# Attention of a two-layer hybrid block: program order on TensorE, maxima steps behind each head's scores, value products in groups of up to four key blocks

## Chip, cores, metric

One core of one Trainium2 chip runs the whole program in one launch. The metric is the time on the device in microseconds (us), the median of the runs shown. A run also has a profile: one execution taken by the hardware profiler, with the start and the duration of every instruction.

The engines are TensorE (PE in the rows; PEld is its weight load), VectorE (DVE), ScalarE (ACT), GpSimd (POOL) and SyncE (SP, which issues the DMAs here). Each works through its own queue in order; semaphores join them.

## What is computed

Two layers over 1024 latent tokens and 256 context tokens, model width 1024, fp32 inputs. Each layer normalizes and modulates its tokens, projects them, runs four head groups side by side (A: latent attention, B: global attention, C: windowed attention with a sink, D: a state-space scan), projects the result back and adds it. The change touches the three attention groups alone. For a block of queries they compute

```python
def one_block(q_blk):
    s = jnp.einsum('bqhgd,bkhd->bhgqk', q_blk, k).astype(jnp.float32) * scale
    p = jax.nn.softmax(s, axis=-1).astype(v.dtype)
    return jnp.einsum('bhgqk,bkhd->bqhgd', p, v)
```

followed by a gate. Context queries read context keys only; latent queries read both (group C reads the context and three neighbouring blocks of 128 keys, with a mask). In the second layer no output is wanted for the context tokens.

## The kernel before, in words

**Pairs and units.** `attention` goes through six pairs of heads in the order B, B, A, A, C, C (`pairs`; `br` is 1, 0 or 2). Each pair is worked in units of query tokens, `GROUPS`: unit 1 (256 to 767), unit 2 (768 to 1279) and, in the first layer only, unit 0 (the 256 context tokens). One call of `main` is one unit.

**A unit.** The keys come in blocks of 128: ten blocks for units 1 and 2 of A and B, seven for those of C, two for unit 0. For each block, `scores` makes the transposed scores of both heads (lines 1215 to 1223: three matmuls per head in A, two in B, three with the mask in C), each in a PSUM tile `ps_st` (tag S2, three buffers), and ScalarE turns each into probabilities `P` (line 1224; the two heads share one tile of the ring `bg`, six buffers, which other work uses too). `add` sums the probabilities over the blocks on GpSimd and VectorE (lines 1240 and 1246). `values` multiplies values by probabilities into `ps_acc` (line 1231): fp32, 64 columns of the array per head, head 0 in columns 0 to 63 and head 1 in columns 64 to 127.

**Order of the value products.** Blocks are gathered in batches of `BATCH` = 2. When a batch is full, the values of the batch *before* it are emitted (`flush_values`), so they lag by one batch; the last batch is emitted by `output` in the next unit.

**Maxima.** The exponential needs each query's largest score, which is computed ahead, by steps that `maxima` returns: `ctx_part` and `lat_part` (`scored`, lines 1143 to 1147: a matmul into `ps_s`, tag MX, three buffers, and a maximum on VectorE into `mp`), and at the end of a query group the step `end`: a reduction into `mt` on VectorE, a transposition `ps_m` on TensorE (line 1171), a copy `ng` on ScalarE and two small DMAs that put the negated maxima as a row into the query tile that line 1217 or 1223 reads. The maxima of units 2 and 0 are made during unit 1; those of the next pair's unit 1, with the loads of that pair (`prep`), during unit 2. These steps are the `pieces` of `main`. They are emitted after each block, evenly, and are to be finished `LEAD` = 2 blocks before the unit's last. In the last pair there are steps `late` besides, which load and split the output weights (`wo`) through the ring `bg`.

**Tail.** After its blocks a unit returns three steps for the next unit to run: `output` (the last values, copy of `ps_acc`, gate), the token sums (eight transpositions `ps_sum`, sixteen instructions on ScalarE, a reciprocal) and `finish` (a transposition `ps_rt`, a DMA out, two back, the product `y`). One is emitted with each batch.

**What sets the order.** The program text is not the order on the engines: a scheduler (the tile framework's) places the instructions of all five engines by its own estimates, as their inputs and buffers come free, and TensorE's queue is a result of that.

Of the kernel before, what the change touches and what calls it, by code (L numbers as in the profile page):

```python
# [24 lines left out]
LEAD = 2  # L25
RD = 2
RD2 = 0
BATCH = 2
N_LATE = 3
AFTER = 3  # L30
X_AT = 0
# [26 lines left out]
def hybrid_block(ctx, tc, x, ctxt, c_t, w_fm, w_tm, w_mod, b_gate, p_col, p_row, w_qu, w_kvu, w_out,  # L58
# [65 lines left out]
    def ps(tag, name=None):  # L124
        return pp.tile([P, 512], F32, tag=tag, bufs=PS_BUFS[tag], name=name or f"ps_{tag}")
# [910 lines left out]
    def attention(L, res, need_ctx, y, late):  # L1036
# [160 lines left out]
        def main(op, gi, pieces, tail):  # L1197
            lo, n = GROUPS[gi]
            nt = n // P
            br, kd = op["br"], op["kd"]  # L1200
            acc = ps("ACC", name="ps_acc")
            sums = [None]
            blocks = key_blocks(br, gi)

            def scores(bi):
                kb, c0, w, mo = blocks[bi]
                k = lambda tok, rows: tok.tile(kb, 0, rows)
                pts = bg((P, 2, 512), name="P")
                for h in range(2):
                    st = ps("S2", name="ps_st")[:, :w]  # L1210
                    q0, q1 = op["q"][h]
                    q = lambda tok, rows: tok(lo + c0, w, 0, rows)
                    if br == 0:
                        k0, k1 = op["k"][h]
                        mm(st, lhsT=k(k0, 96), rhs=q(q0, 96), start=True, stop=False)  # L1215
                        mm(st, lhsT=k(k1, 96), rhs=q(q0, 96), start=False, stop=False)
                        mm(st, lhsT=k(k0, 97), rhs=q(q1, 97), start=False, stop=True)  # L1217
                    else:
                        k0, k1 = op["k"][0]
                        mm(st, lhsT=k(k0, 128), rhs=q(q0, 128), start=True, stop=False)  # L1220
                        if mo is not None:
                            mm(st, lhsT=ident_r, rhs=mask_r[:, mo:mo + w], start=False, stop=False)
                        mm(st, lhsT=k(k1, 65), rhs=q(q1, 65), start=False, stop=True)  # L1223
                    nc.scalar.activation(out=pts[:, h, :w], in_=st, func=AF.Exp, scale=op["scale"])  # L1224
                return pts

            def values(bi, pts):
                kb, c0, w, mo = blocks[bi]
                for h in range(2):
                    v0 = h * 64 if br == 0 else op["pair"] * 64  # L1230
                    mm(acc[h * 64:h * 64 + 64, c0:c0 + w], lhsT=op["v"].tile(kb)[:, v0:v0 + 64], rhs=pts[:, h, :w],  # L1231
                       start=(bi == 0), stop=(bi == len(blocks) - 1))

            def add(bi, pts):
                kb, c0, w, mo = blocks[bi]
                if bi == 0:
                    sums[0] = pts
                elif bi == 1:
                    s = ac((P, 2, 512), name="ac")
                    nc.gpsimd.tensor_tensor(out=s[:, :, :n], in0=sums[0][:, :, :n], in1=pts[:, :, :n], op=ALU.add)  # L1240
                    sums[0] = s
                else:
                    s = sums[0]
                    for h in range(2):
                        eng = nc.vector if h == 0 and bi % 2 == 0 else nc.gpsimd
                        eng.tensor_tensor(out=s[:, h, c0:c0 + w], in0=s[:, h, c0:c0 + w], in1=pts[:, h, :w], op=ALU.add)  # L1246

            todo = []

            def flush_values():  # L1250
                for bi, pts in todo:
                    values(bi, pts)
                todo.clear()

            total, done = len(pieces), 0
            batch = []
            for bi in range(len(blocks)):
                pts = scores(bi)
                batch.append((bi, pts))
                add(bi, pts)  # L1260
                if len(batch) == BATCH or bi == len(blocks) - 1:
                    for _ in range(2 if len(tail) > 3 else 1):
                        if tail:
                            tail.pop(0)()
                    flush_values()
                    todo.extend(batch)
                    batch = []
                want = min(total, -(-total * (bi + 1) // max(1, len(blocks) - LEAD)))
                while done < want:
                    pieces[done]()  # L1270
                    done += 1
            if br == 2:
                for h in range(2):
                    hd = op["pair"] * 2 + h
                    es = tm(name="es")
                    nc.scalar.activation(out=es[64:65, :n], in_=f32(op["q"][h][1](lo, n, 64, 65)), func=AF.Exp,
                                         scale=HEAD_SCALE, bias=pr[64:65, PR_SINK + hd:PR_SINK + hd + 1])
                    nc.vector.tensor_tensor(out=sums[0][64:65, h, :n], in0=sums[0][64:65, h, :n], in1=es[64:65, :n], op=ALU.add)
            o = tm(name="o")
            last_unit = gi == gorder[-1]  # L1280

            def output():
                flush_values()
                nc.scalar.copy(o[:, :n], acc[:, :n])
                nc.gpsimd.tensor_tensor(out=o[:, :n], in0=o[:, :n], in1=op["gate"](lo, n), op=ALU.mult)
                if last_unit:
                    free_all(op["free"])


            ss = small([P, 8], "asum", "asum", 2)  # L1290

            def token_sums(h):
                pss = ps("TR", name="ps_sum")
                for t in range(nt):
                    nc.tensor.transpose(pss[:, t * P:(t + 1) * P], sums[0][:, h, t * P:(t + 1) * P], ident)
                for t in range(nt):
                    junk = tm((P, P), name="junk")
                    nc.scalar.activation(out=junk, in_=pss[:, t * P:(t + 1) * P], func=AF.Copy, scale=2.0,
                                         accum_out=ss[:, h * nt + t:h * nt + t + 1])
                if h == 1:  # L1300
                    nc.vector.reciprocal(out=ss[:, :2 * nt], in_=ss[:, :2 * nt])

            def finish():
                pr_ = ps("TR", name="ps_rt")
                nc.tensor.transpose(pr_[0:2 * nt, 0:P], ss[:, :2 * nt], ident)
                row = tm((8, P), name="rrow")
                nc.scalar.copy(row[0:2 * nt, :], pr_[0:2 * nt, 0:P])
                dr = d_rs[n_unit[0] % 4]
                n_unit[0] += 1
                nc.sync.dma_start(out=dr[0:2 * nt, :], in_=row[0:2 * nt, :])  # L1310
                rb = tm(name="rb")
                for h in range(2):
                    nc.sync.dma_start(out=rb[h * 64:h * 64 + 64, :n],
                                      in_=dr[h * nt:(h + 1) * nt, :].rearrange("t q -> (t q)").unsqueeze(0).to_broadcast([64, n]))
                nc.vector.tensor_tensor(out=y[br * 2 + op["pair"]](lo, n), in0=rb[:, :n], in1=o[:, :n], op=ALU.mult)
            return tail + [output, lambda: [token_sums(h) for h in range(2)], finish]

        sink8 = const([P, 4])
        nc.vector.tensor_scalar(out=sink8, in0=pr[:, PR_SINK:PR_SINK + 4], scalar1=8.0, scalar2=None, op0=ALU.mult)
# [10 lines left out]
        y_slots, tail = [], []  # L1330
        for i, (br, pair) in enumerate(pairs):
            op = ops[br, pair]
            if need_ctx and i == 0:
                pk = Slot([P, 4, NCTX], F32, "y_cx")
                y_slots.append(pk)
            if need_ctx and br == 2:
                pk = res["ssd"].y_slots[0]
            s = Slot([P, NLAT], F32, f"y{br}{pair}")
            y_slots.append(s)
            y[br * 2 + pair] = Tok(pk.t[:, br * 2 + pair - (2 if br == 2 else 0), :] if need_ctx else None, s.t)  # L1340
            for gi in gorder:
                pieces = []
                if gi == 1:
                    for g in gorder[1:]:
                        pieces += maxima(op, g)
                elif gi == 2 and i + 1 < len(pairs):
                    pieces = prep(*pairs[i + 1])
                if i + 1 == len(pairs):
                    pieces = pieces + sum((late() for _ in range(N_LATE)), [])
                tail = main(op, gi, pieces, tail)  # L1350
        while len(tail) > 2:
            tail.pop(0)()
        yield y_slots, tail

# [128 lines left out]
    for L in range(DEPTH):  # L1483
# [48 lines left out]
        y_slots, tail = next(gen[0])  # L1532
# [86 lines left out]
```

## Time and profile before

| | us |
|---|---|
| median of 3 runs | 1849.13 |
| lowest, highest run | 1848.83, 1856.71 |
| profiled execution, its own time | 1844.81 |
| span of its instructions | 1843.0 |
| attention of the first layer in that span | about 545 to 856 |
| attention of the second layer | about 1440 to 1745 |

How to read it: busy time is the time in which an engine has an instruction in flight; a matmul's end is modelled, and matmuls overlap, so that the distance from one start to the next says more of TensorE than durations do. Where the timeline merges equal instructions, "x8" is their count and the duration is that of the whole stretch. In brackets stands the idle time before an instruction, and who ended it. The granted clock is a share of TensorE's 2.4 GHz.

### The profile page before, as it was taken

How to read it: one execution, taken by the hardware profiler on the slowest of the kernel's cores; microseconds unless marked ns; L12 is line 12 of the kernel's file. 1: busy time of each engine (PE TensorE's matmuls, PEld its weight loads, DVE VectorE, ACT ScalarE, POOL GpSimd, SP SyncE). 2: the span in 40 equal slices, each digit the busy share in tenths (PEclk: the TensorE clock that was granted, in tenths of full speed). 3: DMA queues.
4: the chain of work that ended last, by engine and by line, in shares of the span. 5: the costliest groups of instructions: out<-in, count | busy, mean ns of one | idle time of the engine just before them, and what ended most of it. 6: DMA issues, size and time to landing. Idle time of an engine off the chain costs nothing.

```text
span 1843.0 us, 27921 instructions
## 1 busy us (share of the span) xinstructions
PE 1752.4 (95%) x9658; PEld 1329.2 (72%) x9658; DVE 1131.8 (61%) x2290; ACT 744.3 (40%) x2060; POOL 783.3 (43%) x735
## 2 busy tenths in 40 slices
PE   6999999999999999998999989999999999999898
PEld 4667888889975556565787768888998555566576
DVE  6867864373466655447546777753744766645953
ACT  5332433332224545556323333343332445455631
POOL 2322552132327766656224134531332576665522
PEclk9999999999999999999999989999999999999999
DMA  9474323255684332224411524231668623220521
GB/s 312 148 229 134 122 100 119 86 189 178 192 221 117 84 105 74 59 62 128 151 58 40 164 90 148 87 120 70 215 195 249 163 75 88 56 65 12 179 85 58
DMA packets 130397, 231.54 MB, mean 126 GB/s; under 512 B 13784, under 2 KB 74560, under 8 KB 130256
## 3 DMA queue, kind: packets, MB, share of 16 engines
q1 hardware_dynamic: 130256, 229.75, 40.2%
q8 instruction: 77, 1.26, 0.3%
q14 instruction: 64, 0.52, 0.1%
HBM read 161.15 MB, written 68.44 MB: 125 GB/s over the span
## 4 chain that ended last, share of the span: by engine, by line
PE 75%; DVE 11%; DMA 4%; issue 3%; POOL 3%; ACT 2%; SPq 0%; POOLq 0%; DVEq 0%; ACTq 0%
PE ps_acc L1231 10%; PE ps_fm L128 7%; PE ps_fm L130 7%; PE ps_fm L129 7%; PE ps_s L1143 6%; PE ps_o L129 3%; PE ps_o L130 3%; PE ps_o L128 3%; PE ps_st L1220 3%; PE ps_st L1223 3%; PE ps_tm L128 2%; PE ps_tm L130 2%; PE ps_tm L129 2%; PE ps_st L1215 2%; PE ps_st L1217 2%
## 5 line engine op out<-in xcount | busy, mean ns | idle before, releaser
L1246 POOL TENSOR_TENSOR ac<-ac,P 128x512 f32<-128x512 f32 (+3 forms) x248 | 310.8, 1274 | 134.8 <-ACT P L1224 114.5
L1147 DVE TENSOR_REDUCE mp<-ps_s 128x1 f32<-128x512 f32 (+3 forms) x428 | 260.7, 658 | 167.7 <-PE ps_s L1143 154.5
L1224 ACT ACTIVATE P<-ps_st 128x512 f32<-128x512 f32 (+3 forms) x456 | 238.0, 555 | 263.5 <-PE ps_st L1223 102.9
L128 PE MATMUL ps_fm<-hh,wfm_hi 128*128 128x512 f32 x576 | 234.3, 407 | 3.2 <-DVE kb L658 1.9
L130 PE MATMUL ps_fm<-hl,wfm_hi 128*128 128x512 f32 x576 | 231.3, 402 | 1.5 <-POOL hl L403 0.7
L129 PE MATMUL ps_fm<-hh,wfm_lo 128*128 128x512 f32 x576 | 229.9, 399 | 0.0
L128 PE MATMUL ps_tm<-wtm_hi,hh 128*128 128x256 f32 x512 | 146.5, 286 | 0.8 <-ACT va L870 0.6
L129 PE MATMUL ps_tm<-wtm_hi,hl 128*128 128x256 f32 x512 | 145.5, 284 | 0.0
L130 PE MATMUL ps_tm<-wtm_lo,hh 128*128 128x256 f32 x512 | 145.3, 284 | 0.0
L130 PEld LDWEIGHTS ps_fm<-hl,wfm_hi 128*128 128x128 f32 x576 | 109.2, 190 | 27.2 <-POOL hl L403 3.3
L128 PEld LDWEIGHTS ps_fm<-hh,wfm_hi 128*128 128x128 f32 x576 | 109.5, 190 | 26.5 <-ACT hf L399 3.3
L129 PEld LDWEIGHTS ps_fm<-hh,wfm_lo 128*128 128x128 f32 x576 | 109.6, 190 | 19.4 <-issue 0.8
L1240 POOL TENSOR_TENSOR ac<-P 128x1024 f32<-128x1024 f32 (+1 forms) x30 | 65.4, 2180 | 136.7 <-ACT P L1224 133.9
L128 PE MATMUL ps_o<-wo_hi,yh 128*128 128x512 f32 x288 | 113.3, 395 | 2.7 <-ACT yh L1373 2.7
L129 PE MATMUL ps_o<-wo_hi,yl 128*128 128x512 f32 x288 | 113.4, 394 | 0.5 <-DVE yl L1374 0.4
L130 PE MATMUL ps_o<-wo_lo,yh 128*128 128x512 f32 x288 | 112.9, 392 | 0.0
L1231 PE MATMUL ps_acc<-P,vt 128*64 128x512 f32 (+3 forms) x416 | 104.3, 542 | 0.0
L128 PEld LDWEIGHTS ps_tm<-wtm_hi,hh 128*128 128x128 f32 x512 | 98.1, 192 | 3.1 <-issue 1.6
L130 PEld LDWEIGHTS ps_tm<-wtm_lo,hh 128*128 128x128 f32 x512 | 98.2, 192 | 0.7 <-issue 0.4
L129 PEld LDWEIGHTS ps_tm<-wtm_hi,hl 128*128 128x128 f32 x512 | 98.2, 192 | 0.5
L1400 POOL TENSOR_TENSOR xres<-xres,dl 128x512 f32<-128x512 f32 x32 | 41.3, 1290 | 105.5 <-DVE dl L1399 105.5
L1246 DVE TENSOR_TENSOR ac<-ac,P 128x512 f32<-128x512 f32 (+3 forms) x88 | 64.8, 736 | 29.1 <-ACT P L1224 17.6
(345 smaller groups left out, 4150.4 us busy)
## 6 DMA issues: line engine op xcount, KB each, us to landing
wfm_raw<-in_w_fm_dram SPq DMA_DIRECT2D x36, 512.0 KB
wm<-in_w_mod_dram SPq DMA_DIRECT2D x64, 256.0 KB
d_q<-qkhl SPq DMA_DIRECT2D x18, 512.0 KB
wm<-in_w_mod_dram SPq DMA_DIRECT2D x16, 512.0 KB
d_gate<-th SPq DMA_DIRECT2D x32, 256.0 KB
wtm_raw<-in_w_tm_dram SPq DMA_DIRECT2D x16, 512.0 KB
qq<-d_q SPq DMA_DIRECT2D x32, 256.0 KB
wo_raw<-in_w_out_dram SPq DMA_DIRECT2D x16, 512.0 KB
```

The lines of the kernel that those rows point to most:

```text
L128: mm(o, lhsT=lh, rhs=rh, start=first, stop=False)
L129: mm(o, lhsT=ll, rhs=rh, start=False, stop=False)
L130: return mm(o, lhsT=lh, rhs=rl, start=False, stop=last)
L1143: mm(o, lhsT=qh(lo + t * P, P, 0, km), rhs=kh(k0, w, 0, km), start=True, stop=mo is None)
L1147: nc.vector.tensor_reduce(out=dst, in_=p[:, :nu * w].rearrange("p (u k) -> p u k", u=nu), axis=AX.X, op=ALU.max)
L1220: mm(st, lhsT=k(k0, 128), rhs=q(q0, 128), start=True, stop=False)
L1223: mm(st, lhsT=k(k1, 65), rhs=q(q1, 65), start=False, stop=True)
L1224: nc.scalar.activation(out=pts[:, h, :w], in_=st, func=AF.Exp, scale=op["scale"])
L1231: mm(acc[h * 64:h * 64 + 64, c0:c0 + w], lhsT=op["v"].tile(kb)[:, v0:v0 + 64], rhs=pts[:, h, :w], start=(bi == 0), stop=(bi == len(blocks) ...
L1240: nc.gpsimd.tensor_tensor(out=s[:, :, :n], in0=sums[0][:, :, :n], in1=pts[:, :, :n], op=ALU.add)
L1246: eng.tensor_tensor(out=s[:, h, c0:c0 + w], in0=s[:, h, c0:c0 + w], in1=pts[:, h, :w], op=ALU.add)
L1400: (nc.vector if t == ts[-1] else nc.gpsimd).tensor_tensor(out=xt.t[:, js], in0=xt.t[:, js], in1=d, op=ALU.add)
```

## The change

With the change, TensorE executes the instructions of each `main` in the order of the program text (`manual_schedule` for that engine alone); the other four engines are placed by the scheduler as before. The text is rewritten: the maxima steps are emitted after each head's scores (twice per block) rather than after each block; values are no longer held back by a batch, they follow the scores of the last block of their group; groups are as even as they can be at up to four blocks (ten blocks: 4, 3, 3; seven: 4, 3; two: 2); the tail has five steps, two of them empty, of which one is emitted after each block, two if more than five are waiting.

```diff
-BATCH = 2
+BATCH = 4
@@ scores
-            def scores(bi):
+            def scores(bi, between):
                     nc.scalar.activation(out=pts[:, h, :w], in_=st, func=AF.Exp, scale=op["scale"])
+                    between(2 * bi + h + 1)
@@ main
-            todo = []
-
-            def flush_values():
-                for bi, pts in todo:
-                    values(bi, pts)
-                todo.clear()
-
             total, done = len(pieces), 0
-            batch = []
-            for bi in range(len(blocks)):
-                pts = scores(bi)
-                batch.append((bi, pts))
-                add(bi, pts)
-                if len(batch) == BATCH or bi == len(blocks) - 1:
-                    for _ in range(2 if len(tail) > 3 else 1):
-                        if tail:
-                            tail.pop(0)()
-                    flush_values()
-                    todo.extend(batch)
-                    batch = []
-                want = min(total, -(-total * (bi + 1) // max(1, len(blocks) - LEAD)))
+
+            def between(step):
+
+                nonlocal done
+                want = min(total, -(-total * step // (2 * max(1, len(blocks) - LEAD))))
                 while done < want:
                     pieces[done]()
                     done += 1
+
+            nb = -(-len(blocks) // BATCH)
+            ends = [-(-len(blocks) * (b + 1) // nb) - 1 for b in range(nb)]
+            batch = []
+            for bi in range(len(blocks)):
+                pts = scores(bi, between)
+                batch.append((bi, pts))
+                add(bi, pts)
+                for _ in range(2 if len(tail) > 5 else 1):
+                    if tail:
+                        tail.pop(0)()
+                if bi in ends:
+                    for b in batch:
+                        values(*b)
+                    batch = []
@@ output, return of main
-                flush_values()
-            return tail + [output, lambda: [token_sums(h) for h in range(2)], finish]
+            return tail + [output, lambda: None, lambda: [token_sums(h) for h in range(2)], lambda: None, finish]
@@ attention
-                tail = main(op, gi, pieces, tail)
-        while len(tail) > 2:
+                with tc.manual_schedule(engines={mybir.EngineType.PE}):
+                    tail = main(op, gi, pieces, tail)
+        while len(tail) > 4:
             tail.pop(0)()
```

## Rows read from the trace of the kernel before

**Rows 1.** The page, busy time of each engine (share of the span, instructions).
```profile
PE 1752.4 (95%) x9658; PEld 1329.2 (72%) x9658; DVE 1131.8 (61%) x2290; ACT 744.3 (40%) x2060; POOL 783.3 (43%) x735
```
**Rows 2.** Stages: stretch, length, busy of PE, PEld, DVE, ACT, POOL; granted clock, DMA.
```profile
600.00:660.00 60.00, 60.00 (x266) 33.47 (x263) 35.76 (x60) 31.75 (x95) 42.95 (x32) 1.00 0.36 98
1620.00:1680.00 60.00, 60.00 (x282) 36.57 (x279) 27.46 (x49) 30.57 (x90) 38.83 (x30) 1.00 0.09 24
```
**Rows 3.** PE's waits in both attention stretches, the longest of each: us, times, longest.
```profile
PE ps_sum L1295 <- DVE mp L1147: 1.8, 1, 1.8
PE ps_rt L1305 <- DVE asum L1301: 2.7, 2, 1.6
```
**Rows 4.** Timeline of PE: one unbroken group of values, two blocks (start, us, what).
```profile
615.07 1.94 PE L1231 MATMUL ps_acc<-P,vt 128*64 128x512 f32 x8
616.93 0.73 PE L1143 MATMUL ps_s<-kk,qq 128*128 128x512 f32 x2
```
**Rows 5.** Timeline of PE: a group of the same size, broken by two transpositions.
```profile
619.37 0.40 PE L1220 MATMUL ps_st<-qq,kk 128*128 128x512 f32 x1
619.60 0.39 PE L1223 MATMUL ps_st<-ql,k 65*128 65x512 f32 x1
619.92 1.93 PE L1231 MATMUL ps_acc<-P,vt 128*64 128x512 f32 x6
621.78 0.27 PE L1171 MATMUL ps_m<-con,mt 128*8 128x128 f32 x1
...
622.10 1.07 PE L1231 MATMUL ps_acc<-P,vt 128*64 128x512 f32 x2
```
**Rows 6.** Timeline of DVE: maxima, an addition, and the reduction of `end`.
```profile
560.00 1.89 DVE L1147 TENSOR_REDUCE mp<-ps_s 128x1 f32<-128x512 f32 x3 [1.48 <-PE ps_s L1143]
561.81 0.68 DVE L1246 TENSOR_TENSOR ac<-ac,P 128x512 f32<-128x512 f32 x1
562.41 0.68 DVE L1147 TENSOR_REDUCE mp<-ps_s 128x1 f32<-128x512 f32 x1
563.13 0.18 DVE L1166 TENSOR_REDUCE mt<-mp 128x8 f32<-128x24 f32 x1
```
**Rows 7.** Timelines of PE and DVE: from a last maxima matmul to its transposition.
```profile
1513.51 0.50 PE L1143 MATMUL ps_s<-kk,qq 128*128 128x512 f32 x1
...
1515.48 0.27 PE L1171 MATMUL ps_m<-con,mt 128*8 128x128 f32 x1
...
1514.65 0.68 DVE L1315 TENSOR_TENSOR y<-rb,o 128x512 f32<-128x512 f32 x1
```
**Rows 8.** Timeline of ACT: exponentials of both widths, first and last token sum.
```profile
598.30 1.21 ACT L1224 ACTIVATE P<-ps_st 128x256 f32<-128x256 f32 x4 [2.08 <-PE ps_st L1223]
...
1496.31 3.05 ACT L1224 ACTIVATE P<-ps_st 128x512 f32<-128x512 f32 x6 [0.30 <-PE ps_st L1223]
...
1500.56 0.28 ACT L1298 ACTIVATE junk<-ps_sum 128x128 f32<-128x128 f32 x1
...
1502.31 0.34 ACT L1298 ACTIVATE junk<-ps_sum 128x128 f32<-128x128 f32 x1
```
**Rows 9.** Timelines of SP and PE: last load of a pair, its first use.
```profile
616.85 0.57 SPq L1050 DMA_DIRECT2D kl<-d_kr  x1
...
632.65 0.74 PE L1143 MATMUL ps_s<-kh_cx,qh 96*128 96x256 f32 x4
```
**Rows 10.** Last pair: timeline of DVE, and PE's longest wait from 835 to 905.
```profile
858.37 2.87 DVE L1522 TENSOR_TENSOR wo_lo<-wo_raw,wo_hi 128x512 fp32r<-128x512 f32 x2
...
PE ps_sum L1295 <- DVE ac L1278: 5.6, 2, 4.5
```
**Rows 11.** Timeline of PE after a wait, and the stage (columns as in rows 2).
```profile
814.64 1.80 PE L1295 MATMUL ps_sum<-con,ac 128*128 128x128 f32 x8 [1.80 <-DVE mp L1147]
816.37 2.83 PE L1231 MATMUL ps_acc<-P,pk 128*64 128x512 f32 x8
...
816.00:820.00 4.00, 4.00 (x17) 1.62 (x16) 1.36 (x4) 1.92 (x15) 0.98 (x2) 0.72 0.00 0
```

## The prediction

> **What bounds the kernel now.** I read the page first: TensorE is busy 95% of the span, no other engine over 61% [rows 1]. Then the busy time by stages: in attention TensorE is busy in 60.00 of 60.00 us in either layer, at a granted clock of 1.00, that is 2.4 GHz, while VectorE has 27 to 36 us, ScalarE 31, GpSimd 39 to 43 [rows 2]. Then TensorE's waits: 7 rows with 4.3 us in the first layer's attention, 5 rows with 6.7 us in the second's, of each the longest stands in front [rows 3]. So the 616 us of attention last as long as TensorE's queue, and the change can give only what shortens that queue: fewer or cheaper instructions, or less time between them. It takes no matmul away. Last I read the timeline of TensorE start to start, since a full busy share hides how the time is used.
>
> There the queue is dense but not at its best. A score matmul of 512 columns starts 0.23 us after the one before (619.37 to 619.60), but 0.32 us pass ahead of a group of values (619.60 to 619.92) [rows 5]. A group of two blocks takes 1.86 us (615.07 to 616.93) [rows 4] and would be 4 x 0.43 = 1.72 at the spacing of its inner starts (the two heads start together, in four pairs 0.43 us apart, which this row merges into "x8"). So entering and leaving a group costs 0.09 + 0.14, some 0.24 us. And where the scheduler cut a group in two, head 1 of a block runs without head 0: 1.86 us, then two transpositions, then 1.07 us [rows 5], against 1.86 for the whole.
>
> **The change, part by part.** *Groups.* Counted along that timeline there are 69 groups now in the first layer and 70 in the second, 139, whole as in the one row and cut as in the other [rows 4, 5]. With 4, 3, 3 blocks (4, 3 in group C, 2 in unit 0) and nothing between, the first layer has 4 x (3+3+1) + 2 x (2+2+1) = 38, the second 4 x 6 + 2 x 4 = 32: 70. 69 fewer x 0.24 = 16.6 us. *Lone heads.* 27 times a piece with one head alone stands in the queue, 20 of them with 512 columns. Each costs 0.43 us twice, since both heads then go alone: 20 x 0.86 + 7 narrower ones at about half of that = 20 us. In program order nothing can come between the two heads, so all of it goes. *Waits of today*: 11 us, replaced by those below. Gain: 16.6 + 20 + 11 = 47.6 us.
>
> The Trainium skill, TensorEngine Tiling (Array Packing), Key Properties, says that a change of tiling mode drains TensorE; going from 128x128 to 128x64 and back is such a change, and the rows agree that it costs something [rows 4, 5]. It names no price, so the sum goes by the rows.
>
> *The step `end`.* This is the price. Now its transposition is put wherever the scheduler finds room; in program order it stands behind the last maxima matmul, and TensorE waits with everything behind it: scores, values, and so ScalarE's exponentials. From the last maxima matmul to the transposition 1.97 us passed (1513.51 to 1515.48), 0.60 of them because of a product `y` on VectorE in between [rows 7]; that leaves 1.37: matmul 0.4, maximum 0.68, reduction 0.18 and the ways between [rows 6]. Of that TensorE works off what stands between. In the six cases where `end` follows its last maxima matmul directly (unit 1 of the first layer's pairs in A and B, and twice in its last pair), only 0.23 us do. There VectorE is late too: a maximum or an addition takes it 0.61 us (three and one in 560.00 to 562.41) [rows 6], at 1.6 maxima and a quarter of an addition per head 1.1 us, while TensorE needs 0.84 in B (two score matmuls and 1.6 maxima at 0.23) and 1.07 in A. After five heads of a group VectorE is 1.3 us behind in B. So 1.4 (A) to 2.5 us (B), 2.0 on the mean: 12 us. In the other 22, one head's scores (0.47 in B, 0.70 in A) stand between, and mostly two maxima are queued: 1.37 + 0.61 - 0.23 - 0.5 to 0.7, some 1.0: 22 us. Bounds: 0.6 and 1.9 for each of the 28, 17 to 53 us.
>
> *Three buffers of maxima.* Within a group's scores TensorE can be three maxima, 1.8 us, ahead of VectorE [rows 6]. Eight heads in B are 8 x (1.1 - 0.84) = 2.1 us behind, less the token sums' transpositions that fall there. I take 2 us in all; bounds 0 and 22 (0.7 in each of 32 stretches of scores in A and B).
>
> *Unit 0, six times.* Its four exponentials take 1.21 us [rows 8], its scores at 256 columns about half of that, and no lag of a batch covers them now: 0.6 us each, 3.6; bounds 0 and 4.
>
> *Tail.* Token sums come after block 2, `finish` after block 4, with an empty step between: 16 instructions on ScalarE take 2.1 us (1500.56 to 1502.65) [rows 8], one block and a group of values of 2.7 us and more are longer: nothing. After unit 0 two steps are taken per block, and one block (1.6 us) stands between the sums and `ps_rt`: 0.7 us, five times, 3.5; bounds 0 and 8. `finish`'s three DMAs go to SP's queue a block earlier; what waits for them is a product on VectorE off the path.
>
> *Loads.* `prep` comes after the first head; its loads go by free slots, and one pair's last stands 15.8 us ahead of its first use [rows 9]. Nothing; half a unit (12 us) of lead would have to be lost before it costs. The DMAs of `ng` have two blocks and a group of values, over 4.5 us, ahead of their reader; nothing.
>
> *Last pair.* VectorE splits output weights there (2.87 us for two) and TensorE's sums wait for the sink's addition behind it, 4.5 us at the longest [rows 10]. In order that holds up scores too: 3 us more; bounds 0 and 8.
>
> *Clock.* At 814.64 TensorE had been idle for 1.80 us; the group behind took 2.76 us instead of 1.86 and the stretch 816 to 820 shows a granted clock of 0.72 [rows 11], so the lower level, 1.2 GHz, for part of it. One such fall more, 1.7 us; bounds 0 and 14 (eight waits near 2 us).
>
> Sum of costs: 34 + 2 + 3.6 + 3.5 + 3 + 1.7 = 47.8; gain 47.6; net +0.2 us. On the profiled execution's 1844.81 us, whose span of 1843.0 leaves 1.8 around it, that is 1845.0. The median of the runs lies 4.3 us above that execution: 1849.3, so **1849 us**: no change that can be told.
>
> **The rivals.** *A, faster: the waits are covered.* If VectorE meets the last maxima idle, a wait is 1.37 - 0.23 - 0.5 = 0.6 us: 28 x 0.6 + 7 for the rest = 24 us, net -24: 1825. For it: VectorE is busy 46 to 60% of the stage, and each group of values (2.7 or 3.6 us without a maximum) lets it catch up [rows 2, 4]. Against it: two maxima are mostly emitted in the step ahead of `end`.
>
> *B, slower: VectorE falls behind in each stretch of scores.* Now its maxima are fed between groups of two blocks; with four blocks in a row the three buffers fill and TensorE, in order, stands. It decides from the point where VectorE's lag passes 1.8 us: with an addition that waits for GpSimd, or a `y` of 0.6 us, in a stretch. Then 32 x 0.7 = 22 us come on top, less the 2 counted: 1849 + 20 = 1869. For it: 2.1 us of lag in eight heads of B; against it: A has none. The Trainium skill, TensorE: Matmul & The Clock Gate, Part 3, states that matmuls start and end strictly in the order of the program, so no later one can slip past a waiting one; the rows here show no exception. Its Part 1 states that an idle array falls back to 1.2 GHz; each such fall is 1.7 us [rows 11], which would push this case to the upper bound.
>
> *C: the order does not hold what it says*, groups are still cut by work from outside `main`. Then the waits are filled as now, and half of the groups' 16.6 and of the lone heads' 20 us is gained: 1849 - 18 = 1831.
>
> **How the numbers follow.** Forecast 0.37, A 0.28, B 0.30, C 0.05. About 0.5%, 9 us, is what a measurement of this kernel can tell from no change. A and C are faster by more, B slower by more: 0.33, 0.37, 0.30. Low end: gain 47.6 against 17 + 2 of costs, 1849 - 28 = 1821. High end: B with five more falls of the clock, 1869 + 5 x 1.7 = 1877. So 1821 to 1877; the forecast's own range is 1840 to 1858.
>
> **What would show it.** Groups "x12" to "x16" of values on TensorE, about 70, none with "x2"; idle time ahead of `ps_m` whose releaser is `mt`, 28 us or more in sum; idle time ahead of `ps_s` from `mp` (B) near 2 or 20 us; a granted clock under 1.00 within attention; scores of unit 0 followed by a gap. I am wrong if `ps_m` does not wait (A), or if TensorE's idle time in attention passes 60 us (B).

## The result, and the profile after

The changed kernel takes 1880.22 us (median of four runs, 1879.48 to 1882.64) against 1850.53 for the kernel before beside it: a ratio of 1.0161, 95% interval 1.0139 to 1.0182. It is slower by about 30 us. The prediction was 1849 with a range up to 1877; direction and size were both missed.

The page of the changed kernel, its span, the busy times, and the granted clock in 40 slices:

```profile
span 1880.7 us, 27918 instructions
PE 1742.3 (93%) x9658; PEld 1345.2 (72%) x9658; DVE 1138.1 (61%) x2290; ACT 749.1 (40%) x2060; POOL 776.2 (41%) x735
PEclk9999999999999999998999989999999999999899
```

Against [rows 1], TensorE is busy for 10 us less in a span that is 37.7 us longer, and the clock has two more slices under 9. (The two profiled executions lie further apart than the medians do, 37.7 us against 29.7: the one before is a quick one of its kernel, 1844.81 us, the one after is the slowest of its four.) The busy time by stages says where. First before, then after; each row is one layer's attention, from the last `ps_fm` matmul ahead of it to the first `ps_o`, and PEclk is the granted clock:

```profile
core 0: us, PE busy (x) PEld busy (x) DVE busy (x) ACT busy (x) POOL busy (x), PEclk, DMA share, GB/s
541.80:876.90 335.10, 322.38 (x1529) 195.04 (x1527) 204.60 (x350) 176.01 (x538) 213.08 (x159) 0.99 0.35 95
1435.70:1744.70 309.00, 300.73 (x1366) 176.72 (x1365) 202.07 (x316) 154.84 (x437) 197.74 (x148) 0.99 0.31 84
```

```profile
544.90:906.50 361.60, 319.63 (x1528) 200.09 (x1526) 212.27 (x349) 178.51 (x538) 205.67 (x159) 0.95 0.32 86
1469.10:1783.20 314.10, 287.50 (x1369) 182.02 (x1368) 202.35 (x319) 158.67 (x443) 197.48 (x148) 0.97 0.31 86
```

The first layer's attention is 26.5 us longer, the second's 5.1: 31.6 of the 37.7 us. (The other 6 lie outside attention and were not followed.) In these two stages TensorE's busy time falls by 16.0 us and its idle time rises from 21.0 to 68.6, by 47.6. So there is a gain in work, and a larger loss in waiting.

TensorE's waits in the same two stages of the changed kernel, first layer and then second (us in total, times, longest); they answer to [rows 3]:

```profile
PE ps_m L1171 <- DVE mt L1166: 16.2, 10, 3.1
PE ps_m L1171 <- DVE mt L1169: 10.9, 6, 2.5
PE ps_sum L1295 <- DVE ac L1279: 4.5, 2, 2.5
PE ps_st L1223 <- DMA ql<-ng: 2.1, 1, 2.1
...
PE ps_sum L1295 <- DVE ac L1279: 8.6, 3, 4.2
PE ps_m L1171 <- DVE mt L1166: 6.1, 8, 1.5
PE ps_m L1171 <- DVE mt L1169: 5.2, 4, 1.8
PE ps_st L1223 <- DMA ql<-ng: 2.2, 1, 2.2
```

The transposition of `end` (`ps_m`) waits 38.4 us in sum. Before, it waited 1.2 us in both stages, 0.5 in the first layer and 0.7 in the second, most of it here:

```profile
PE ps_m L1171 <- DVE mt L1169: 0.5, 1, 0.5
PE ps_m L1171 <- DVE mt L1166: 0.4, 1, 0.4
```

One of the longest waits after, in the timeline, VectorE first, then TensorE:

```profile
562.86 0.88 DVE L1247 TENSOR_TENSOR ac<-ac,P 128x512 f32<-128x512 f32 x1
563.66 2.47 DVE L1147 TENSOR_REDUCE mp<-ps_s 128x1 f32<-128x512 f32 x4
566.18 0.69 DVE L1247 TENSOR_TENSOR ac<-ac,P 128x512 f32<-128x512 f32 x1
566.79 0.17 DVE L1166 TENSOR_REDUCE mt<-mp 128x8 f32<-128x24 f32 x1
```

```profile
563.65 0.40 PE L1143 MATMUL ps_s<-kk,qq 128*128 128x512 f32 x1
567.11 0.37 PE L1171 MATMUL ps_m<-con,mt 128*8 128x128 f32 x1 [3.06 <-DVE mt L1166]
567.13 0.78 PE L1220 MATMUL ps_st<-qq,kk 128*128 128x512 f32 x1
...
568.26 5.15 PE L1232 MATMUL ps_acc<-P,vt 128*64 128x512 f32 x12
573.35 0.50 PE L1220 MATMUL ps_st<-qq,kk 128*128 128x512 f32 x1
```

TensorE has issued its last maxima matmul at 563.65, when VectorE has four maxima (2.47 us), an addition and the reduction still to do. It stands for 3.06 us. And what comes behind is slow: the group of twelve values takes 5.15 us, while the same group elsewhere takes 2.79:

```profile
1524.10 2.79 PE L1232 MATMUL ps_acc<-P,vt 128*64 128x512 f32 x12
```

The transposition has a wait of 2.96 us at 632.00, and these two stand in the pairs of A:

```profile
697.31 0.27 PE L1171 MATMUL ps_m<-con,mt 128*8 128x128 f32 x1 [2.45 <-DVE mt L1166]
...
764.65 0.37 PE L1171 MATMUL ps_m<-con,mt 128*8 128x128 f32 x1 [2.44 <-DVE mt L1166]
```

The granted clock from 563, behind the wait at 632.00, and behind the last two (same columns as the stages):

```profile
563.00:567.10 4.10, 1.05 (x5) 0.55 (x4) 3.91 (x7) 1.11 (x2) 2.67 (x3) 0.89 0.28 97
567.10:573.00 5.90, 5.89 (x15) 1.75 (x15) 0.00 (x0) 0.86 (x2) 1.26 (x1) 0.50 0.44 105
...
631.90:638.00 6.10, 6.00 (x15) 1.78 (x15) 0.43 (x1) 0.86 (x2) 1.26 (x1) 0.51 0.06 12
...
697.50:703.50 6.00, 5.59 (x26) 2.60 (x25) 2.17 (x3) 1.83 (x4) 2.07 (x2) 1.00 0.07 23
765.10:772.00 6.90, 6.90 (x18) 2.22 (x18) 0.67 (x1) 0.74 (x2) 1.26 (x1) 0.57 0.35 90
```

From 567.10 to 573.00 the granted clock is 0.50, the lower level of 1.2 GHz. Of these four direct waits, three are followed by such a stretch (behind 567, 632 and 765), one is not (697). The last pair has two more direct waits, of 2.52 us at 868.50 and 1.62 at 871.22, and from 870.00 to 876.80 the clock is 0.50 there too. Over the whole execution the mean granted clock fell from 0.990 to 0.974. Since the lower level is half the upper, that is (1 - 0.974) x 2 x 1880.7 = 98 us at 1.2 GHz against 37 before. (The kernel before had 0.982 to 0.990 in its other executions, 0.985 or 0.986 in the middle, so 37 is its low end.) For the two attention stages alone the same sum gives 55 us after (0.05 x 2 x 361.6 + 0.03 x 2 x 314.1) and 13 before; both are estimates, since the clocks are given to two digits.

### The profile page after: what moved, and what is told of

It is laid out like the page before. It is cut to its first block, busy times and chain, and to the rows that moved or that the text cites. A ratio compares the mean times of both kernels' runs of the same rounds, so it can differ in the third digit from the quotient of the medians.

```text
span 1880.7 us, 27918 instructions
## 1 busy us (share of the span) xinstructions
PE 1742.3 (93%) x9658; PEld 1345.2 (72%) x9658; DVE 1138.1 (61%) x2290; ACT 749.1 (40%) x2060; POOL 776.2 (41%) x735
## 4 chain that ended last, share of the span: by engine, by line
PE 70%; DVE 15%; DMA 5%; issue 4%; POOL 4%; ACT 2%; SPq 0%; POOLq 0%; DVEq 0%; ACTq 0%
PE ps_acc L1232 10%; PE ps_fm L128 6%; PE ps_fm L130 6%; PE ps_fm L129 6%; PE ps_s L1143 4%; PE ps_o L128 3%; PE ps_o L130 3%; PE ps_o L129 3%; DVE mp L1147 3%; PE ps_st L1220 3%; PE ps_st L1223 2%; PE ps_st L1215 2%; PE ps_st L1217 2%; PE ps_st L1216 2%; PE ps_tm L128 2%
## 5 line engine op out<-in xcount | busy, mean ns | idle before, releaser
L1247 POOL TENSOR_TENSOR ac<-ac,P 128x512 f32<-128x512 f32 (+3 forms) x248 | 300.5, 1228 | 182.5 <-ACT P L1224 112.7
L1224 ACT ACTIVATE P<-ps_st 128x512 f32<-128x512 f32 (+3 forms) x456 | 243.5, 559 | 248.5 <-PE ps_st L1223 115.7
L1247 DVE TENSOR_TENSOR ac<-ac,P 128x512 f32<-128x512 f32 (+3 forms) x88 | 77.2, 877 | 52.4 <-ACT P L1224 36.4
L1232 PE MATMUL ps_acc<-P,vt 128*64 128x512 f32 (+3 forms) x416 | 88.3, 558 | 0.0
```

## The experiments

The theory, W: the loss is TensorE standing in program order ahead of `ps_m`, plus the lower clock that those waits leave behind. The rivals: K, only the waits cost, the clock does not; S, program order merely moves the wait, VectorE is late anyway; T, the rewritten text (no lag of a batch, four blocks of scores in a row) is what costs.

### `end` later

The transposition, its copy and its DMAs become a step of their own, emitted three heads' scores after the reduction:

```diff
-            return r + [end]
+            turn.late = 3
+            return r + [end, turn]
...
+                while held and (held[0][0] <= step or step == 2 * len(blocks) - 1):
+                    held.pop(0)[1]()
```

> The changed kernel, but each transposition of `end` (with its copy and its two DMAs) is emitted three heads' scores after the reduction it reads. Theory W (the loss is the 38 us that TensorE stands in program order ahead of ps_m, and what those waits do to the clock): the waits ahead of ps_m fall from 38 us to under 6, the half-clock stretches behind three of the first layer's direct ones (3 x 6.8 us, some 10 us lost) go, and the time is 1880 - 33 - 10 = 1837. Rival K (the waits alone, the clock costs nothing that matters): 1847. Rival S (program order moves the wait on: VectorE is late anyway, and TensorE stands ahead of ps_s or ps_st instead): the time stays at 1865 to 1880, with new waits of 20 us or more.

Measured: 1831.71 us, ratio to the kernel before 0.9904 (0.9871 to 0.9937), 48.5 us faster than the changed kernel. The same two stages:

```profile
541.10:869.90 328.80, 307.28 (x1528) 196.52 (x1527) 225.08 (x352) 176.87 (x538) 214.02 (x159) 0.97 0.35 95
1432.50:1731.10 298.60, 282.50 (x1369) 180.06 (x1368) 209.61 (x315) 156.97 (x441) 200.59 (x148) 0.98 0.33 90
```

And the waits of the first layer:

```profile
PE ps_m L1175 <- DVE mt L1166: 3.0, 2, 2.2
PE ps_m L1175 <- DVE mt L1169: 1.5, 3, 0.8
```

`ps_m` waits 4.5 us here and 0.3 in the second layer, in place of 38.4, and little took their place: idle time fell by 31.0. Beside it the two stages lose 17.3 us of busy time, with the same matmuls. By their granted clocks 32 us of them are at the lower level, where the changed kernel has 55; half of the difference, some 12 us, is an estimate of what the clock gave back, and the rest of the 17.3 was not traced. W holds, within 6 us of its number; K, at 1847, and S fall.

### Only the six direct ones later

As above, for group 2's `end` in the first layer alone:

```diff
-            turn.late = 3
+            turn.late = 3 if need_ctx and gi == 2 else 0
```

> The changed kernel, but only the six transpositions of `end` that follow their last maxima matmul directly (group 2's, first layer) are emitted three heads' scores later. Their waits are 11.5 us in four pairs (3.22, 3.12, 2.60, 2.60). Theory W: these waits go and so do the three half-clock stretches behind them (3 x 6.8 us, 10 us lost): 1880 - 11.5 - 10 = 1858. Rival K (no price of the clock): 1868. Rival S: 1875 to 1880.

Measured: 1860.88 us, ratio 1.0069 (1.0047 to 1.0092). The first layer's waits ahead of `ps_m` fall from 27.1 to 15.4 us:

```profile
PE ps_m L1175 <- DVE mt L1166: 7.9, 6, 2.3
PE ps_m L1175 <- DVE mt L1169: 7.5, 4, 2.4
```

11.7 us of waits went, and the time fell by 19.3, so 7.6 us more than the waits. That is W's number (1858) within the interval, and K's (1868) outside it. Six of 28 steps carry 19.3 of the 48.5 us. (Five of the six stand directly behind their last maxima matmul; the one of the fifth pair waits 1.70 us behind one head's scores, and the sixth direct one is group 0's in the last pair, left as it was.)

### The wait filled with work

The changed kernel with ten extra matmuls ahead of the same six transpositions. They compute nothing that is used; the transposition overwrites them.

```diff
+                if need_ctx and gi == 2:
+                    for _ in range(10):
+                        mm(pm, lhsT=ident_r, rhs=mask_r[:, 0:512], start=True, stop=True)
                 nc.tensor.transpose(pm[0:2 * nt, 0:P], mt[:, :2 * nt], ident)
```

> The changed kernel, with ten extra 512-column matmuls (2.2 us, their result is overwritten) just ahead of the same six transpositions: the wait is kept as time, but TensorE works in it. Theory W: the three half-clock stretches behind these waits go, the waits left are under 1 us: 1880 - 10 = 1870, with the same product and values otherwise. Rival K: 1880 to 1884, since the extra work only fills the wait.

Measured: 1871.63 us, ratio 1.0120 (1.0081 to 1.0159): 8.6 us faster than the changed kernel with 60 matmuls more. All four of its runs (1868.34 to 1874.00) are below all four of the changed kernel, but the two intervals overlap, so the verdict rests on the place itself. TensorE's timeline there:

```profile
559.05 2.44 PE L1173 MATMUL ps_m<-mask_r 128*128 128x512 f32 x10
562.23 0.27 PE L1174 MATMUL ps_m<-con,mt 128*8 128x128 f32 x1 [0.74 <-DVE mt L1166]
562.26 0.48 PE L1223 MATMUL ps_st<-qq,kk 128*128 128x512 f32 x1
...
562.91 2.79 PE L1235 MATMUL ps_acc<-P,vt 128*64 128x512 f32 x12
565.63 0.50 PE L1223 MATMUL ps_st<-qq,kk 128*128 128x512 f32 x1
```

and its granted clock:

```profile
562.23:568.30 6.07, 5.11 (x25) 2.29 (x25) 1.45 (x3) 2.06 (x4) 2.43 (x2) 1.00 0.40 115
```

The transposition comes 3.18 us after the first of the ten (559.05 to 562.23), which is 3.41 after the last maxima matmul at 558.82; in the changed kernel it was 3.46 (563.65 to 567.11). So the delay is the same, but the clock stays at 1.00 and the group takes 2.79 us. From the first score matmul behind the transposition to the one behind the values it is 3.37 us here (562.26 to 565.63) and 6.22 in the changed kernel (567.13 to 573.35): one fall of the clock costs 2.85 us in this place. Three of them are 8.6 us, which is what the medians gained; the runs spread over 5.7 us, so that the figures meet so closely is in part luck. In the first layer the waits ahead of `ps_m` fall from 27.1 to 13.1 us, and the extra matmuls put 14.6 us (six times 2.44) in their place, so the gain is not in the waits. This is the price of the clock with the delay left in.

### Groups of two

```diff
-BATCH = 4
+BATCH = 2
```

> The changed kernel with groups of two key blocks: about 118 groups in place of 68. If a group costs 0.24 us to enter and leave, as the sum had it: +50 x 0.24 = 12 us, 1892. Rival B (long stretches of scores let VectorE fall behind, and TensorE stands for it): shorter stretches give back 10 to 20 us of waits, 1860 to 1880.

Measured: 1918.93 us, ratio 1.0370 (1.0334 to 1.0406): 38.7 us slower, three times the 12. The longest new wait, VectorE and then TensorE:

```profile
1528.65 1.47 DVE L1315 TENSOR_TENSOR y<-rb,o 128x512 f32<-128x512 f32 x1
1530.04 1.74 DVE L1247 TENSOR_TENSOR ac<-ac,P 128x512 f32<-128x512 f32 x1
1531.71 1.28 DVE L1147 TENSOR_REDUCE mp<-ps_s 128x1 f32<-128x512 f32 x2
...
1533.34 0.27 PE L1171 MATMUL ps_m<-con,mt 128*8 128x128 f32 x1 [4.21 <-DVE mt L1166]
```

With the groups elsewhere, the tail's product `y` and an addition (1.47 and 1.74 us, each more than twice the 0.68 of [rows 6, 7]) fall just ahead of the last maxima. In both stages the waits ahead of `ps_m` are 52.2 us in sum, where the changed kernel has 38.4. So this run mixes the price of groups with another position of `end`, and could not give the first. The control is the kernel with `end` later and groups of two:

> e1_end_later with groups of two: the price of groups alone, with no `end` in the way. At 0.24 us for entering and leaving a group: 1831.7 + 50 x 0.24 = 1844. If e4's 38.7 us were all the groups' own (0.77 us each): 1870. Between them, the part that e4 lost at `end` is what 1870 leaves out.

Measured: 1846.40 us, ratio 0.9984 (0.9969 to 0.9998): 14.7 us over the same kernel with groups of four. By the text there are 118 groups in place of 70, so 48 more and not 50, and each costs 0.31 us; given the spread of the runs (1843.45 to 1853.32 here) the estimate of 0.24 held. The other 24 of the 38.7 us are not lost once `end` is out of the way.

### The order and the text apart

The changed text without `manual_schedule`:

```diff
-                with tc.manual_schedule(engines={mybir.EngineType.PE}):
-                    tail = main(op, gi, pieces, tail)
+                tail = main(op, gi, pieces, tail)
```

> The changed kernel's text (maxima behind each head, groups of up to four) without the program order: the scheduler places TensorE's instructions as in the kernel before. Theory W (the loss sits in the order, at `end`, not in the rewritten text): ps_m waits go back under 5 us, the groups are cut again in part, and the time is near the kernel before, 1840 to 1855. Rival T (the text is what costs: values no longer lag a batch, four blocks of scores in a row): 1865 to 1880 even without the order.

Measured: 1840.11 us, ratio 0.9953 (0.9926 to 0.9980). And the reverse edit in the kernel before, with nothing else changed:

> The kernel before with nothing changed but the program order on TensorE: groups of two, lagging a batch, maxima after each block's two heads. Theory W: the groups are whole (118 in place of 139: 5 us less, and 20 us of lone heads less), but `end` waits in order as in the changed kernel, with some 38 us and 15 us of clock: 1850 - 25 + 53 = 1878. Rival T (the rewritten text is what costs, the order only gains): 1825 to 1835.

Measured: 1904.65 us, ratio 1.0286 (1.0259 to 1.0313). Waits of the first layer in this kernel:

```profile
PE ps_m L1171 <- DVE mt L1166: 16.8, 11, 1.9
PE ps_rt L1305 <- DVE asum L1301: 13.9, 6, 3.5
PE ps_m L1171 <- DVE mt L1169: 9.4, 6, 2.2
```

The text alone gains half a per cent; the order alone loses 55 us. T falls. With `end` later, the new text in program order (1831.71) is 8 us ahead of the same text placed freely, and the two intervals overlap a little; free placement with `end` later was not run. The old text loses 27 us more in order than expected. Half of that stands ahead of `ps_rt`, 13.9 us: `finish` too comes right behind what it waits for. With the new text, which has an empty step there, the changed kernel waits 1.1 us for it in the first layer.

### The waits that are left

Four runs went after what remains at 1832. In the last pairs the sink's addition was put behind block 1, away from the splitting of output weights on VectorE, and the last block's addition went to GpSimd:

```diff
                     sums[0] = s
+                    if br == 2:
+                        sink()
...
-                        eng = nc.vector if h == 0 and bi % 2 == 0 else nc.gpsimd
+                        eng = nc.vector if h == 0 and bi % 2 == 0 and (br < 2 or bi < len(blocks) - 1) else nc.gpsimd
```

> e1_end_later, and in the last pairs (branch 2) the sink's exponential and its addition on VectorE come behind block 1 instead of at the unit's end, and the last block's addition goes to GpSimd: what the token sums wait for no longer stands behind the splitting of output weights. Left in e1 there: waits ahead of ps_sum of 18.4 us in six places, and 37 us at half clock in and behind the last pairs, some 10 of which must stay. Theory W: 10 to 15 us of waits and 5 to 10 of clock go: 1832 - 20 = 1812. Rival S (VectorE and GpSimd are late there anyway and the wait moves to another operand): 1827 to 1832.

Measured: 1832.62 us, ratio 0.9901 (0.9876 to 0.9926): nothing. `ps_sum` no longer waits for the sink, but others do, as in the second layer:

```profile
PE ps_rt L1328 <- DVE asum L1324: 4.1, 1, 4.1
PE ps_acc L1237 <- ACT P L1229: 1.9, 1, 1.9
```

Here S is right: moving one operand moves the wait, in the longer of the two rows to another product of VectorE. Taking the weights' copies off VectorE instead, with `end` later and the sink where it was:

```diff
-                    nc.vector.tensor_copy(st[1].t[:, js], st[0][:, js])
+                    nc.scalar.copy(st[1].t[:, js], st[0][:, js])
```

> e1_end_later, with the upper half of the output weights copied on ScalarE in place of VectorE in the last pairs. TensorE waits 17 us there ahead of ps_sum for the sink's addition, queued on VectorE behind these copies (0.37 us each) and subtractions (0.65). Theory W (these waits cost what they last, and the clock behind them): a third of VectorE's queue goes, 6 us of waits and a fall or two: 1823. Rival S (another operand is late too, as in e7, where ps_rt took over 10 us): 1829 to 1833.

Measured: 1837.44 us, ratio 0.9931 (0.9916 to 0.9946), no gain either, and above what either theory gave. In the first layer's last pairs VectorE has 61.31 us of work in 90 in place of 68.81 (first row: `end` later; second: this kernel), TensorE the same:

```profile
785.00:875.00 90.00, 76.17 (x440) 54.82 (x439) 68.81 (x132) 55.44 (x211) 47.47 (x40) 0.91 0.31 97
790.00:880.00 90.00, 76.39 (x439) 55.18 (x438) 61.31 (x111) 61.02 (x218) 44.70 (x40) 0.91 0.32 100
```

Why the sums still wait with VectorE relieved was not settled. Then the first unit of each layer, with four maxima ahead of its scores:

```diff
+            if first:
+                for _ in range(4):
+                    work[done]()
+                    done += 1
```

> e1_end_later, with four maxima of the next group put ahead of the scores in the first unit of each layer, where TensorE waits 2.4 and 2.3 us for the DMA of ng and stands at half clock for 3.4 us behind it. Theory W: the four maxima fill the wait and the clock stays up there: 1831.7 - 4.7 - 2 x 1.7 = 1824. Rival S (work only moves, or the maxima hold TensorE by VectorE): 1830 to 1834.

Measured: 1827.41 us, ratio 0.9895 (0.9869 to 0.9920), between the two theories and not told apart from 0.9904. In the first layer the maxima came before the transposition, and the wait for `ng` stayed:

```profile
541.36 0.50 PE L1228 MATMUL ps_st<-ql,kk_cx 65*128 65x512 f32 x1 [2.13 <-DMA ql<-ng]
```

Yet the clock did not fall there in the profiled execution: it is 1.00 from 538 to 549, where the kernel with `end` later has 0.84 in its first 11 us (541 to 552). In the second layer both have 0.84.

All of these together, and `turn.late = 4`:

> e7_sink_early with both of these and with `end` four heads' scores later in place of three. Theory W: the pieces add up, since the first unit and the last pair lie apart: 1832 - 8 (first unit) - 8 (ps_rt and ps_acc behind VectorE) - 3 (the 2.3 us left ahead of ps_m and its half clock) = 1813. Rival S: only the first unit counts, 1824.

Measured: 1826.10 us, ratio 0.9873 (0.9858 to 0.9887): the lowest median of this study, 23 us under the kernel before and 54 under the changed one. Of the 54, 48.5 come from moving `end` alone. W's sum of the pieces (1813) did not come; S, with 1824, was near.

## Why the prediction was wrong

*What it got right.* Values stand in 40 and 32 groups (38 and 32 predicted). A group costs 0.31 us (0.24). The rewritten queue is shorter by about what was summed: with `end` out of the way the two stages are busy 33.3 us less than before, though with more of them at the lower clock; 36.6 was predicted for groups and lone heads. The 22 `end` steps behind one head's scores wait 1.06 us each (38.4 less 15.05 for the six direct ones, by 22), where 1.0 was predicted.

*The step that failed: the clock.* The prediction took "one such fall more, 1.7 us", with a bound of 14, though it had the mechanism in its rows [rows 11]: TensorE idle for 1.80 us, then a slow group. It forecast six waits near 2 us and eight in its bound, yet let only one of them lower the clock. The runs give 2.85 us for one fall in a group of twelve, three of them behind the direct waits of B and A alone, and in the two attention stages together some 55 us at the lower level against 13 before. Half of the 42 us more, some 21, is by this estimate the size of the term that was put at 1.7. (The 1.7 itself is sound for one fall, but not from [rows 11] alone: 816 to 820 at 0.72 gives 1.1, and the stretch ahead of it, 812 to 816, which had 0.85, the other 0.6.) The Trainium skill, TensorE: Matmul & The Clock Gate, Part 1, which the prediction cited for a rival only, says that an idle array goes back to 1.2 GHz; the trace agrees (0.50 behind a wait of 3.06 us), and the filled wait shows it (1.00 in the same place).

*The direct waits.* 2.0 us on the mean was too short: in the timeline the six are 3.06, 2.96, 2.45, 2.44, 2.52 and 1.62, 2.5 on the mean. The prediction let three buffers of maxima hold TensorE at most three ahead of VectorE. At 563.65 four maxima were unread, so TensorE had not been held; the lag all arrived at `end`, with an addition on top. That is 3 us over six steps. For the same reason rival B, which had the sign and at 1869 was nearest, had the wrong mechanism: waits ahead of `ps_s` by maxima, 1.3 us in both stages, were not what cost. TensorE's idle time did pass the 60 us that the prediction had named as the sign of B (68.6), but it stands ahead of `ps_m`.

*Small terms.* A wait of 2.1 and 2.2 us for `ng` in each layer's first unit was put at nothing: "two blocks and a group of values" do not lie ahead there, because the maxima of that unit come from the stage before. The waits ahead of `ps_sum` in both stages rose from 9.8 to 14.5 us (3 more were predicted).

Put together for the two stages: busy time fell by 16.0 us, which with some 21 us for the lower clock (1.7 forecast) leaves some 37 us less work (36.6 forecast); idle time rose by 47.6 us where the terms came to 35.1 (34 + 2 + 3.6 + 3.5 + 3, less the 11 of the kernel before). So of the 31.4 us between the net of 31.6 and the 0.2 forecast, some 19 are the clock and 12.5 idle time; of these 12.5, 3 are the direct waits, 4.3 those for `ng`, 1.7 the sums, and the remainder was not taken apart.

## What to carry to other kernels

When a queue is put in program order, look for every instruction that stands right behind the thing it waits for, and ask what its releaser has queued ahead at that moment; moving six or 28 of them three heads' scores later was worth 19 and 48 us, while the reordering had made TensorE's work 33 us shorter. Price a wait on TensorE twice, once for its length and once for the slow matmuls behind it, and if the trace shows one such fall, let every wait of that length carry the chance of one. A control that keeps the wait but fills it with work tells the two prices apart.

## What the runs showed of the hardware

Two waits of 2.45 and 2.44 us in the same kernel, behind the same kind of work, went different ways: after the first the granted clock stayed at 1.00, after the second it was 0.57. So the price of a wait of this length is not the same each time, and a sum can only take it as a chance: of the four direct waits in B and A, three paid it.
